# A two-block transformer program on one core: 28 weight pieces of the second block split ahead of time on POOL

## The chip, the core and the metric

The kernel runs on one core of one Trainium2 chip. The metric is the device time of one execution in microseconds (us). Five engines work side by side and wait for each other through semaphores: PE (TensorE: matrix products), DVE (VectorE: element-wise work), ACT (ScalarE: element-wise work and function tables), POOL (GpSimd: element-wise work, and transfers of its own) and SP (SyncE: only starts transfers). Each engine takes its instructions strictly in the order in which the built program holds them.

## What is computed

512 tokens with 1024 channels go through a first block of two layers (mixer, cross-attention, feed-forward with a convolution, each followed by a residual and a layer norm) and then through a second block. The second block, cut to what matters here:

```python
def second_block(x, c, norm_g, w_ada, b_ada, w_in, ...):
    mod = silu(c) @ w_ada + b_ada
    shift, scale, gate = split(mod, 3)
    h = rms_norm(x, norm_g) * (1 + scale) + shift
    proj = h @ w_in                      # r, k, v, g, wd+ad | q, ka, va, g_a
    ps = token_shift(proj[..., :D_SHIFT], mu_shift)
    y_r, g_r = rwkv7_mix(ps, ...)        # 8 heads, a state per head, 512 steps
    y_a = chunk_band_attention(q, ka, va, ...)
    y = concat(y_r * silu(g_r), y_a * silu(g_a))
    return x + gate * (y @ w_out)
```

All inputs are float32. A float32 product is made of three products of rounded parts: hi\*hi, hi\*lo and lo\*hi, where hi is the value cast to the engine's 32-bit format `fp32r` and lo is the value minus hi. So each weight has to be split into hi and lo before PE can use it.

## The kernel before

A weight matrix is cut into pieces of 128 x 1024 numbers (0.5 MB). `piece` (line 239) brings one in: SP loads it into a `raw` tile, ACT casts it to hi (line 229), and DVE, or in the second block POOL, subtracts to get lo (line 230). Hi and lo lie together in a tile `w` of 128 x 2 x 1024 (1 MB) from a ring of four; the first block has more rings (`rawx`, `wx`). A piece feeds 24 products of 512 columns (lines 263 to 265, three for each of 8 groups of channels).

The feed-forward stage `ffn` (line 619) runs over three chunks of hidden channels: 8, 8 and 6 blocks "up" (two pieces each), each followed by 8 blocks "down" (one piece each). In it DVE makes the splits of the weights and of the hidden values `hd`, and POOL has nothing to do until the residual's sums (`res_stat`, lines 370 and 371) at the end of the third chunk.

The second block has one line of work with long waits, and much other work for PE. The line is, for each of four pairs of heads, `rwkv_pair` (line 866), then the inversion of small triangular matrices `rwkv_invert` (line 990), then the chain of states `rwkv_chain`. The other work stands in the list `ORDER` (line 48): an entry is a milestone and a name, `r5` being piece 5 of the matrix `in_r`, `q17` the same for queries and keys, `g` the gates, `v0` and `v1` two passes over the four pieces of the values. `fill(us)` takes that much of it from the list wherever the line would wait; work of a later milestone isn't touched before the line has got there. Pieces 16, 0, 4, 8 and 1 (`OPEN`) are multiplied already in `open2`, ahead of the second block; `ORDER` names piece 1 once more as `r1`.

In `rwkv_pair` DVE works with POOL on the same tiles: line 904 (a scan) and 889 on DVE, 905 on POOL, 921, 892, 913 and 894 on DVE, 914, 919, 915 and 919 on POOL, then 918 on DVE. A PE product on the result of line 894 (line 897; it is recorded at line 834, that of the helper `mm`) follows, then transposes (837), the scores within the chunks (834), DVE's masks (960) and line 971. In `rwkv_invert` DVE runs 31 steps of two small instructions (lines 1003 and 1005), each on the result of the last, and then the result goes out to HBM and back (lines 1007 to 1020) before line 1027 turns it. The normalisation of queries and keys (lines 348 to 350, 1160, with a PE product at 1157) is mixed into these steps.

What follows is printed by a program, with the lines of the profile:

Of the kernel before, what the change touches and what calls it, by code (L numbers as in the profile page):

```python
# [172 lines left out]
class Prog:  # L173
# [69 lines left out]

    def raw(self):
# [7 lines left out]
    def wtile(self):  # L252
        """The weights' ring: some of its room is there only in the first block."""
# [13 lines left out]
    def lin(self, src, ms, xs, epi, n=S, first=0, last=0):  # L267
        """The first (last) few blocks go through one half of the tokens, then through the other, for the LN
        before (after) them; epi(m, psum, tokens) gets the last ones by halves."""
# [43 lines left out]
    def flush(self):  # L313
        """The LN that is due."""
# [6 lines left out]
    def lin_tm(self, src, pieces, xs, ntok, epi):  # L321
        """out[tok tiles][128, 512 cols]: activations stationary, weights moving."""
# [20 lines left out]
    def rsqrt(self, y, t, v, eps):  # L343
        """y = (v + eps) ** -0.5: the table's value and a Newton step; eps is a column of self.eps."""
# [7 lines left out]
    # residual, then LN over the channels  # L352
# [61 lines left out]
    # mixer of layer 0  # L414
# [204 lines left out]
    def ffn(self, l, xs):  # L619
        nc = self.nc  # L620
        for c, (f0, f1) in enumerate(CHUNKS):
# [3 lines left out]
            def epi(m, ps, ts):  # L625
# [9 lines left out]
                else:  # L635
                    h = self.tmp()
                    nc.vector.tensor_tensor(out=h, in0=ps, in1=keep["g"], op=ALU.mult)
                    hs.append(self.split(self.hd(), h))

# [5 lines left out]
            def epi_d(m, ps, ts):  # L645
# [5 lines left out]
                if c == 1 and l == 0 and m == 1:  # L651
                    self.ada_end()
                if c == 2:
                    self.res_stat(m, ts)
# [5 lines left out]
    # the modulation of the second block, gathered a piece at a time  # L660
# [23 lines left out]
    def ada_end(self):  # L684
        nc = self.nc
        # the sum over the partitions: within 32 of them by turning 32-blocks, then over the four groups
# [18 lines left out]
    def modulate(self, ts):  # L705
        """rms_norm(x) * norm_g * (1 + scale) + shift of half of the tokens."""
# [16 lines left out]
    def open2(self):  # L723
        """The second block's first products, of the first half of the tokens."""
# [48 lines left out]
    # The second block has one line of work with long waits (the states) and much other work for the tensor  # L773
    # engine: `bg` holds the latter as generators, and fill() puts some of it wherever the former waits.
# [57 lines left out]
    def mm(self, out, **kw):  # L832
        """A product on the line with the waits: it stays behind what fill() put before it."""
        self.tc.keep_in_program_order(self.nc.tensor.matmul(out, **kw))  # L834
# [4 lines left out]
    def lin_g(self, src, m, xs, epi, ks=range(KT)):  # L839
        w = self.piece(self.a[src][m])  # L840
# [25 lines left out]
    def rwkv_pair(self, j):  # L866
        """What the chunks of heads 2j and 2j+1 need."""
# [9 lines left out]
        # kk  # L877
# [12 lines left out]
        # k'  # L890
        nc.scalar.activation(u, av, AF.Identity, bias=self.ka1[:, j : j + 1], scale=self.v("k_a_2", j))
        nc.vector.tensor_tensor(out=k, in0=k, in1=u, op=ALU.mult)
        # bonus
# [7 lines left out]
        # decays  # L901
# [469 lines left out]
```

## Time and profile before

| | us |
|---|---|
| median of 3 runs | 1854.24 |
| the runs | 1853.18 to 1855.95 |
| the profiled execution (its span) | 1854.5 |
| PE busy | 1786.7 (96%) |
| DVE busy | 1096.3 (59%) |
| ACT busy | 783.0 (42%) |
| POOL busy | 362.8 (20%) |

The second layer's feed-forward stage lies between 1047 and 1430 us of the span, the four pairs between 1460 and 1600, the inversion between 1600 and 1661, and the chain of states and the output after that. A row of a timeline gives the start, the duration, the engine, the line, the operation, the output and input tiles, and in square brackets how long the engine had been idle and what ended that.

### The profile page before, as it was taken

To read this page: it belongs to the slowest core of one execution; us is meant where nothing else is said; L and a number is where in the kernel's file an instruction comes from. 1 tells how busy PE (TensorE), PEld (TensorE's weight loads), DVE (VectorE), ACT (ScalarE), POOL (GpSimd) and SP (SyncE) were. 2 spreads that over 40 slices of the span, in tenths; PEclk is the share of its full clock that TensorE was granted. 3 is DMA by queue.
4 is the path that set the end of the run, shared out by engine and by line. 5 is a ranking of instruction groups with operands and counts; after the bars stand their busy time and mean duration, and the time that the engine had idled before them with its cause. 6 is when DMAs were issued, how large, how long until landed. Compare 5 with 4: busy or idle time off the path is not lost.

```text
span 1854.5 us, 26344 instructions
## 1 busy us (share of the span) xinstructions
PE 1786.7 (96%) x10476; PEld 1502.4 (81%) x10476; DVE 1096.3 (59%) x1741; ACT 783.0 (42%) x1319; POOL 362.8 (20%) x331
## 2 busy tenths in 40 slices
PE   8999998999999999999999999999998888879999
PEld 7889988888888888988998988888887766656657
DVE  5676689743463467444565764343447666975673
ACT  5444534532332356232453642232335645535561
POOL 0115014000000051000501400000015455623232
PEclk9999999999999999999999999999999999989999
DMA  8431455332322226333131242323222222222142
GB/s 279 145 103 60 132 181 188 100 102 91 102 92 91 80 64 196 112 96 100 59 104 35 69 125 92 102 92 100 88 86 73 82 75 88 89 74 81 56 160 103
DMA packets 62635, 192.25 MB, mean 104 GB/s; under 512 B 7344, under 2 KB 10032, under 8 KB 62512
## 3 DMA queue, kind: packets, MB, share of 16 engines
q1 hardware_dynamic: 54432, 172.25, 29.0%
q0 software_dynamic: 3248, 9.44, 1.5%
q10 hardware_dynamic: 4832, 8.88, 1.4%
q8 instruction: 82, 1.34, 0.3%
q14 instruction: 41, 0.34, 0.1%
HBM read 181.36 MB, written 9.18 MB: 103 GB/s over the span
## 4 chain that ended last, share of the span: by engine, by line
PE 76%; DVE 15%; ACT 3%; issue 3%; DMA 2%; POOL 0%; SPq 0%; DVEq 0%; ACTq 0%; POOLq 0%
PE ch L264 10%; PE ch L263 10%; PE ch L265 10%; PE mm L263 9%; PE mm L265 9%; PE mm L264 9%; PE pv L264 3%; PE pv L263 3%; PE pv L265 3%; PE ch L834 3%; DVE x L401 2%; DVE xh L405 1%; DVE w L230 1%; DVE x L400 1%; DVE vt L681 1%
## 5 line engine op out<-in xcount | busy, mean ns | idle before, releaser
L263 PE MATMUL mm<-xh,w 128*128 128x512 f32 (+1 forms) x704 | 266.1, 378 | 8.5 <-ACT w L229 7.5
L265 PE MATMUL mm<-xh,w 128*128 128x512 f32 (+1 forms) x704 | 258.6, 367 | 0.8 <-DVE w L230 0.8
L264 PE MATMUL mm<-xh,w 128*128 128x512 f32 (+1 forms) x704 | 259.0, 368 | 0.0
L370 POOL TENSOR_TENSOR t<-x,x 128x512 f32<-128x512 f32 x6 | 8.1, 1351 | 1011.1 <-ACT w L229 656.1
L229 ACT CAST w<-raw 128x1024 fp32r<-128x1024 f32 (+2 forms) x131 | 133.1, 1017 | 164.0 <-PE ch L265 62.9
L263 PEld LDWEIGHTS mm<-xh,w 128*128 128x128 f32 x704 | 135.6, 193 | 35.7 <-ACT w L229 7.8
L264 PE MATMUL ch<-xh,w 128*128 128x512 f32 (+1 forms) x432 | 154.1, 357 | 0.6 <-DVE xh L405 0.5
L264 PEld LDWEIGHTS mm<-xh,w 128*128 128x128 f32 x704 | 135.9, 193 | 22.9 <-issue 3.4
L263 PE MATMUL ch<-xh,w 128*128 128x512 f32 (+1 forms) x432 | 153.0, 354 | 1.3 <-ACT xh L404 1.3
L265 PE MATMUL ch<-xh,w 128*128 128x512 f32 (+1 forms) x432 | 152.7, 353 | 1.5 <-DVE w L230 1.5
L265 PEld LDWEIGHTS mm<-xh,w 128*128 128x128 f32 x704 | 135.8, 193 | 22.6 <-issue 1.1
L229 ACT CAST wx<-raw 128x1024 fp32r<-128x1024 f32 (+1 forms) x85 | 88.1, 1039 | 152.4 <-PE ch L265 71.5
L230 DVE TENSOR_TENSOR w<-rawx,w 128x1024 fp32r<-128x1024 f32 (+2 forms) x85 | 104.1, 1225 | 68.0 <-ACT w L229 67.6
L229 ACT CAST w<-rawx 128x1024 fp32r<-128x1024 f32 (+2 forms) x85 | 87.3, 1027 | 116.4 <-PE mm L265 71.0
L230 DVE TENSOR_TENSOR w<-raw,w 128x1024 fp32r<-128x1024 f32 (+2 forms) x90 | 113.0, 1257 | 37.8 <-ACT w L229 37.4
L230 DVE TENSOR_TENSOR wx<-raw,wx 128x1024 fp32r<-128x1024 f32 (+1 forms) x85 | 107.6, 1267 | 27.6 <-ACT wx L229 27.4
L230 POOL TENSOR_TENSOR w<-raw,w 128x1024 fp32r<-128x1024 f32 x41 | 100.4, 2456 | 119.0 <-ACT w L229 115.1
L263 PE MATMUL ch<-xh,wx 128*128 128x512 f32 (+1 forms) x304 | 103.5, 341 | 0.0
L265 PE MATMUL ch<-xh,wx 128*128 128x512 f32 (+1 forms) x304 | 103.0, 339 | 0.0
L264 PE MATMUL ch<-xh,wx 128*128 128x512 f32 (+1 forms) x304 | 103.0, 339 | 0.0
L263 PE MATMUL mm<-hd,w 128*128 128x256 f32 (+1 forms) x304 | 97.7, 322 | 3.6 <-ACT hd L229 3.6
L265 PE MATMUL mm<-hd,w 128*128 128x256 f32 (+1 forms) x304 | 97.9, 322 | 0.0
(484 smaller groups left out, 4498.6 us busy)
## 6 DMA issues: line engine op xcount, KB each, us to landing
raw<-in_up SPq DMA_DIRECT2D x56, 512.0 KB, 3.5
rawx<-in_up SPq DMA_DIRECT2D x32, 512.0 KB, 3.5
kt<-in_ada SPq DMA_DIRECT2D x48, 256.0 KB, 3.3
raw<-in_dn SPq DMA_DIRECT2D x24, 512.0 KB, 3.5
raw<-in_in_r SPq DMA_DIRECT2D x24, 512.0 KB, 3.5
raw<-in_c_in SPq DMA_DIRECT2D x16, 512.0 KB, 3.5
raw<-in_xo SPq DMA_DIRECT2D x12, 512.0 KB, 3.6
raw<-in_xv SPq DMA_DIRECT2D x11, 512.0 KB, 4.1
```

Source lines behind the costliest of these rows:

```text
L229: nc.scalar.copy(hi, src)
L230: (eng or nc.vector).tensor_tensor(out=lo, in0=src, in1=f32(hi), op=ALU.subtract)
L263: mm(out, lhsT=ah, rhs=bh, start=start, stop=False)
L264: mm(out, lhsT=ah, rhs=bl, start=False, stop=False)
L265: mm(out, lhsT=al, rhs=bh, start=False, stop=stop)
L370: eng.tensor_tensor(out=sz, in0=self.x[0][:, ts] if m == 1 else sz, in1=z, op=ALU.add)
L400: (nc.vector if k in DVE_SUB else nc.gpsimd).tensor_tensor(out=x, in0=x, in1=mn, op=ALU.subtract)
L401: nc.vector.scalar_tensor_tensor(out=x, in0=x, scalar=gk, in1=rs, op0=ALU.mult, op1=ALU.mult)
L405: nc.vector.scalar_tensor_tensor(out=lo, in0=x, scalar=bk, in1=f32(hi), op0=ALU.add, op1=ALU.subtract)
L681: nc.vector.scalar_tensor_tensor(out=dst, in0=raw, scalar=sc, in1=dst, op0=ALU.mult, op1=ALU.add)
L834: self.tc.keep_in_program_order(self.nc.tensor.matmul(out, **kw))
```

## The change

1. `r1` is taken out of `ORDER`: piece 1 of `in_r` is multiplied once (in `open2`), not twice.
2. `pre_begin`, at the start of the second layer's feed-forward, lists 28 pieces in the order of `ORDER`: those of `r`, `q` and `g` that are left and the four of `v0`.
3. `pre_step` takes one of them, after each hidden block and after each "down" block of the first two chunks (32 calls). POOL copies one column of the tile just made by DVE into the new tile (which makes POOL wait for that point of the stage), starts the load, casts to hi, subtracts to lo, and starts the store of hi and lo (1 MB) to HBM. There are two tiles for it, under the tag `vt`, which cross-attention has finished with by then.
4. `ready` takes the place of `piece` in `lin_g`, `att_v`, `out_begin` and `out_end`: if the piece was prepared, SP loads the 1 MB straight into the `w` tile, and neither ACT nor POOL touches it. The pieces of the output matrix weren't prepared and go through `piece` as before.

```diff
 ORDER = (
-    (0, "r1"), (0, "r5"), (0, "r9"),
+    (0, "r5"), (0, "r9"),
...
+    def pre_step(self, at):
+        nc = self.nc
+        if self.todo:
+            key = self.todo.pop(0)
+            t = self.t("vt", [P, 2, D], F32, 2)
+            nc.gpsimd.tensor_copy(t[:, 1, 0:1], at[:, 0:1])
+            nc.gpsimd.dma_start(out=t[:, 1, :], in_=self.a[key[0]][key[1]])
+            self.due2.append((key, t))
+        if len(self.due2) > 1 or not self.todo:
+            for key, t in self.due2[:1]:
+                self.due2.pop(0)
+                hi, lo = t[:, 0, :].bitcast(F32R), t[:, 1, :].bitcast(F32R)
+                nc.gpsimd.tensor_copy(hi, t[:, 1, :])
+                nc.gpsimd.tensor_tensor(out=lo, in0=t[:, 1, :], in1=t[:, 0, :], op=ALU.subtract)
...
+                d = self.prep[key] = self.dram.tile([P, 2, D], F32, tag=name, name=name)
+                nc.gpsimd.dma_start(out=d, in_=t)
...
+    def ready(self, src, m):
+        if (src, m) not in self.prep:
+            return self.piece(self.a[src][m])
+        w = self.wtile()
+        self.nc.sync.dma_start(out=f32(w), in_=self.prep[src, m])
+        return w
...
@@ ffn
                     hs.append(self.split(self.hd(), h))
+                    if l == 1:
+                        self.pre_step(f32(hs[-1][:, 0, :]))
...
+                if c < 2 and l == 1:
+                    self.pre_step(x)
...
@@ lin_g
-        w = self.piece(self.a[src][m])
+        w = self.ready(src, m)
```

POOL in the second pair of heads. `w` and `raw` are a piece and its source; `rt`, `rk`, `ar` and `c` are the pair's own tiles; `yd` and `dn` are in HBM. Before:

```order
L230 TENSOR_TENSOR w_12628<-raw_12627,w_12628 128x1024
L905 TENSOR_TENSOR rt_12460<-rt_12462,rt_12460 128x512
L230 TENSOR_TENSOR w_12667<-raw_12666,w_12667 128x1024
L914 TENSOR_TENSOR ar_12520<-rk_12297,rt_12516 128x8x64
L919 TENSOR_TENSOR c_1638_12521<-rk_12349,rt_12462 64x8x64
L915 TENSOR_TENSOR rt_12484<-rt_12484,rt_12461 128x512
L919 TENSOR_TENSOR c_1638_12521<-rk_12349,rt_12462 64x8x64
L230 TENSOR_TENSOR w_12690<-raw_12689,w_12690 128x1024
L900 DMA yd<-rt_12463 128x512
```

The same place on POOL after the change (lines 905, 914, 919, 915, 900 and 966 are now 952, 961, 966, 962, 947 and 1013):

```order
L952 TENSOR_TENSOR rt_12615<-rt_12617,rt_12615 128x512
L961 TENSOR_TENSOR ar_12672<-rk_12408,rt_12668 128x8x64
L966 TENSOR_TENSOR c_1658_12673<-rk_12490,rt_12617 64x8x64
L962 TENSOR_TENSOR rt_12636<-rt_12636,rt_12616 128x512
L966 TENSOR_TENSOR c_1658_12673<-rk_12490,rt_12617 64x8x64
L947 DMA yd<-rt_12618 128x512
L1013 DMA dn<-mk_1600_12387 32x8x32 x4
```

The three subtractions of weight pieces are gone from among the pair's own five instructions.

PE in the first pair of heads, from the product on line 894's result on: `mm_12359` is a filler product of `r9`, `at` and `ch` are the scores. Before:

```order
L834 MATMUL ch_12271<-rt_12225,cst 128x512
L837 MATMUL ch_12314<-cst,rk_12207 64x128
L834 MATMUL ch_12314<-cst,rk_12207 64x64
L837 MATMUL ch_12314<-cst,rk_12207 128x128 x3
L837 MATMUL ch_12332<-cst,rk_12207 128x128 x4
L264 MATMUL mm_12359<-xh_11312,w_12355 128x512
L265 MATMUL mm_12359<-xh_11312,w_12355 128x512
L263 MATMUL mm_12359<-xh_11313,w_12355 128x512
```

The same place on PE after the change (834 and 837 are now 881 and 884):

```order
L881 MATMUL ch_12464<-rt_12421,cst 128x512
L884 MATMUL ch_12504<-cst,rk_12403 64x128
L881 MATMUL ch_12504<-cst,rk_12403 64x64
L884 MATMUL ch_12504<-cst,rk_12403 128x128 x3
L884 MATMUL ch_12522<-cst,rk_12403 128x128 x4
L881 MATMUL at_12545<-ar_12475,c_1624_12476 128x128
L881 MATMUL ch_12544<-ar_12475,c_1624_12476 128x128
```

Eight filler products stood between the transposes and the first scores, and 18 more between and after the scores; now there are none, and 7 after the scores. Ahead of this place 45 filler products stand where 46 stood.

SP at the beginning of the second block. Before:

```order
L241 DMA raw_12469<-in_in_r 128x1024
L241 DMA raw_12540<-in_in_r 128x1024
L241 DMA raw_12596<-in_in_va 128x1024
L241 DMA raw_12627<-in_in_va 128x1024
L241 DMA raw_12666<-in_in_va 128x1024
```

The same place on SP after the change (`sp_...` is a prepared piece in HBM):

```order
L282 DMA w_12495<-sp_in_r_9528 128x2048
L282 DMA w_12624<-sp_in_r_9605 128x2048
L282 DMA w_12692<-sp_in_r_9682 128x2048
L282 DMA w_12745<-sp_in_va_9759 128x2048
L282 DMA w_12773<-sp_in_va_9836 128x2048
```

The loads go straight into the ring `w`, so a load waits until PE has left the tile; before it waited until POOL had left one of two `raw` tiles.

## Rows read from the trace of the kernel before

**Rows 1.** The page: busy time of each engine, its share of the span, instructions.

```profile
PE 1786.7 (96%) x10476; PEld 1502.4 (81%) x10476; DVE 1096.3 (59%) x1741; ACT 783.0 (42%) x1319; POOL 362.8 (20%) x331
```

**Rows 2.** Busy time of each engine in stretches (the clock is 1.00 at 2.4 GHz).

```profile
core 0: us, PE busy (x) PEld busy (x) DVE busy (x) ACT busy (x) POOL busy (x), PEclk, DMA share, GB/s
0.00:46.00 46.00, 37.77 (x235) 35.28 (x236) 25.23 (x43) 24.44 (x37) 0.51 (x5) 0.96 0.83 278
1060.00:1300.00 240.00, 239.39 (x1114) 199.05 (x1113) 111.72 (x133) 83.11 (x107) 0.00 (x0) 1.00 0.31 99
1460.00:1600.00 140.00, 120.30 (x687) 87.71 (x686) 99.52 (x140) 72.64 (x103) 85.92 (x57) 0.93 0.25 79
1600.00:1661.00 61.00, 50.21 (x200) 37.11 (x196) 53.80 (x94) 23.20 (x33) 24.33 (x21) 0.89 0.31 96
1661.00:1855.00 194.00, 186.47 (x1558) 126.81 (x1557) 107.79 (x325) 91.49 (x218) 46.93 (x36) 1.00 0.28 97
```

**Rows 3.** What PE waited for from 1437 us on: total, times, longest.

```profile
PE ch L834 <- DVE rt L894: 17.8, 4, 4.9
PE at L1157 <- ACT t L1153: 6.0, 2, 5.8
PE ch L834 <- DVE rt L1027: 3.3, 1, 3.3
```

**Rows 4.** PE's timeline in the first pair: fillers, then the product on line 894.

```profile
1465.42 0.40 PE L263 MATMUL mm<-xh,w 128*128 128x512 f32 x1
...
1474.28 0.39 PE L263 MATMUL mm<-xh,w 128*128 128x512 f32 x1
1479.34 1.47 PE L834 MATMUL ch<-rt,cst 128*128 128x512 f32 x2 [4.67 <-DVE rt L894]
```

**Rows 5.** DVE's timeline in the second pair and, last row, in the fourth.

```profile
1503.87 2.25 DVE L921 COPY pc<-rt 128x8 f32<-128x8 f32 x1
1506.04 0.68 DVE L892 TENSOR_TENSOR rk<-rk,rt 128x512 f32<-128x512 f32 x1
...
1508.31 2.96 DVE L894 SCALAR_TENSOR_TENSOR rt<-rk,vec,rk 128x512 f32<-128x512 f32 x1
...
1581.44 2.68 DVE L892 TENSOR_TENSOR rk<-rk,rt 128x512 f32<-128x512 f32 x1
```

**Rows 6.** POOL's timeline at the same places.

```profile
1503.23 2.86 POOL L230 TENSOR_TENSOR w<-raw,w 128x1024 fp32r<-128x1024 f32 x1
1506.04 1.79 POOL L914 TENSOR_TENSOR ar<-rk,rt 128x512 f32<-128x512 f32 x1
...
1580.74 2.83 POOL L230 TENSOR_TENSOR w<-raw,w 128x1024 fp32r<-128x1024 f32 x1
```

**Rows 7.** DVE's lines 349 and 1003 from 1600 to 1652 (min/median/max ns), and two timelines.

```profile
L349 DVE TENSOR_SCALAR t<-t x5: 420/428/4366, 1604.4 to 1651.3; 128x512 f32<-128x512 f32 x5
...
L1003 DVE TENSOR_TENSOR rt<-c,c x31: 191/374/2514, 1609.4 to 1646.9; 128x31 f32<-128x31 f32 x2, 128x60 f32<-128x60 f32 x2, 128x87 f32<-128x87 f32 x2, 128x112 f32<-128x112 f32 x2
...
1610.95 2.33 DVE L1003 TENSOR_TENSOR rt<-c,c 128x87 f32<-128x87 f32 x1
...
1610.74 4.79 POOL L230 TENSOR_TENSOR w<-raw,w 128x1024 fp32r<-128x1024 f32 x2 [2.28 <-ACT w L229]
```

**Rows 8.** Groups of instructions from 1437 us on (first row), and from 1060 to 1300.

```profile
L230 POOL TENSOR_TENSOR w<-raw,w 128x1024 fp32r<-128x1024 f32 x40 | 97.8, 2454 | 118.1 <-ACT w L229 114.3 <-DMA raw<-in_in_r 3.5
...
L230 DVE TENSOR_TENSOR w<-raw,w 128x1024 fp32r<-128x1024 f32 x16 | 19.6, 1223 | 3.7 <-ACT w L229 3.7
...
L230 DVE TENSOR_TENSOR hd<-t,hd 128x512 fp32r<-128x512 f32 x16 | 11.0, 685 | 0.7 <-ACT hd L229 0.7
```

**Rows 9.** Transfers: SP's queue from 1060 to 1300; KB and us to landing from 1437.

```profile
q1 hardware_dynamic: 6480, 23.60, 30.6%
...
raw<-in_in_r SPq DMA_DIRECT2D x18, 512.0 KB, 3.5
...
dt<-c POOLq DMA_DIRECT2D x1, 512.0 KB, 2.9
```

More of the change, by code (lines that the diff above doesn't have):

```diff
@@ L242, in piece, with pre_begin @@
         return self.split(w, raw[:, :cols], cols, None if self.extra else self.nc.gpsimd)
+    def pre_begin(self):
+        self.prep, todo = {}, []
+        for _, ws in ORDER:
+            for w in ws.split("+"):
+                k, m = w[0], int(w[1:])
+                if k in "rq" and m not in OPEN:
+                    todo.append(("in_r", m))
+                elif k == "g":
+                    todo.append(("in_r", 12 + m) if m < 4 else ("in_ga", m - 4))
+                elif w == "v0":
+                    todo += [("in_va", i) for i in range(4)]
+        self.todo, self.due2 = todo, []
+    def pre_step(self, at):
[12 more added lines that the diff above has]
+                nc.gpsimd.tensor_tensor(out=lo, in0=t[:, 1, :], in1=t[:, 0, :], op=ALU.subtract)
+                name = f"sp_{key[0]}{key[1]}"
+                d = self.prep[key] = self.dram.tile([P, 2, D], F32, tag=name, name=name)
[6 more added lines that the diff above has]
+        return w
     def raw(self):
@@ L620, in ffn @@
         nc = self.nc
+        if l == 1:
+            self.pre_begin()
         for c, (f0, f1) in enumerate(CHUNKS):
@@ L638, in epi @@
                     hs.append(self.split(self.hd(), h))
+                    if l == 1:
+                        self.pre_step(f32(hs[-1][:, 0, :]))
             self.lin(f"up{l}", [o + f for f in range(f0, f1) for o in (NF, 0)], xs, epi, first=FIRST if c == 0 else 0)
@@ L1133, in att_v @@
         for jj in range(4):
-            w = self.piece(self.a["in_va"][jj])
+            w = self.ready("in_va", jj)
             for kk in range(2):
@@ L1257, in out_begin @@
         for m in range(NPART):
-            w, ps = self.piece(self.a["out"][m]), self.bank(("mm", "mm", "ch", "ch")[m])
+            w, ps = self.ready("out", m), self.bank(("mm", "mm", "ch", "ch")[m])
             self.part.append((w, ps))
@@ L1276, in out_end @@
             else:
-                w, ps = self.piece(self.a["out"][m]), self.bank()
+                w, ps = self.ready("out", m), self.bank()
                 for k in range(KT):
```

## The prediction

> **What bounds the kernel now.** I read the busy times first: PE works 96% of the span and no other engine comes near [rows 1], so time can only go where PE is idle, slow, or does work it need not do. The stretches show where that is [rows 2]. In the second layer's feed-forward (1060 to 1300) PE has no gap and POOL does nothing. In the four pairs (1460 to 1600) PE is idle for 140.0 - 120.3 = 19.7 us, in the inversion (1600 to 1661) for 10.8 us. After 1661 it is nearly full until the output's last pieces, which the change doesn't touch. The granted clock fell in just these two stretches, behind the waits: a mean of 0.93 over 140 us is a loss of 9.8 us of full-speed work, 0.89 over 61 us one of 6.7 us; each is time at the level of 1.2 GHz in place of 2.4. Idle time and clock together are 47 us, the most that any cure of the waits could bring.
>
> Then what ended the waits [rows 3]: four times DVE's line 894, at most 4.9 us each, once each in a pair; in the inversion ACT's line 1153 (5.8 us) and line 1027. All belong to the line of work in the second block, none to a weight piece. So pieces arrive in time already, and the split can matter only by what it does to DVE and ACT. The timelines show that it does: DVE's line 921, a copy of eight columns, took 2.25 us and ended at 1506.12, when POOL's split of a weight piece ended at 1506.09 [rows 5, 6]. Line 892 took 0.68 us in the second pair, but 2.68 in the fourth, where such a split ran from 1580.74 on. In the inversion a step of 87 columns took 2.33 us beside two splits, where the median step, a longer one, takes 0.374 [rows 7]. DVE stands still for as long as POOL works on a piece. POOL does this 40 times from 1437 us on, 2.45 us each [rows 8]; the change leaves the 8 pieces of the output matrix.
>
> **The change part by part.** *Piece r1.* 24 products go. Fillers follow each other every (1474.28 - 1465.42)/39 = 0.227 us [rows 4], so PE has 5.4 us less. They go from the first pair: behind the product on line 894, 7 fillers stand where 26 stood. Ahead of it the number is the same, so nothing of this is lost in the wait. But what follows (masks, line 971) is DVE's own line, and with fewer fillers PE may meet it: between 2 and 5.4 us, I take 4.4, since the splits that held DVE there are gone too.
>
> *The splits leave the pairs.* One split per pair stands between line 904 and line 894: ahead of line 921 in three pairs, of line 892 in the fourth. Each costs the line about 2.0 us (2.68 - 0.68 for line 892; for line 921 2.25 less a small copy, near the 0.191 of the smallest step in [rows 7]). POOL's own lines stay, and line 914 moves up into the place of the split: it took 1.79 us against 2.86 [rows 6], so at least 2.86 - 1.79 = 1.07 us is gained, at most 2.86. I take 2.0, four times: 8 us (4.3 to 11.4). Each is less than its wait, so all of it shows, and POOL's lines 919 and 915, inside line 894's 2.96 us, are next late: they stay.
>
> *The splits leave the inversion.* Five of the 62 steps took 2.3 to 2.6 us, 12.2 us together, where five median ones take 5 x 0.37: 10.4 us too long. Line 349 took 4.37 us ahead of the first step, 0.43 in the median [rows 7]: 3.9 us. The steps form one chain, so 14.3 us can go. PE's work up to line 1027's products is 163 fillers, 163 x 0.227 = 37 us, and a few small products, in a stretch of 61, so PE doesn't bound this before the chain does. The result's way through HBM (2.9 us out [rows 9], as much back) now runs beside loads of 1 MB. If each way took 2.9 us longer, 8.5 would be left; and if the port went to others in half the cases, 5. I take 12 (5 to 14.3); the 5.8 us behind ACT's line 1153 goes with it, since ACT stood there behind DVE.
>
> *The clock.* Of the 16.5 us, what follows waits that become short comes back. Waits of line 894 shrink from 4.9 to some 2.5 us; whether the clock then falls, no row tells: 0 to 10 us, and I take 4.
>
> *Work for POOL in the feed-forward.* Each piece adds a cast and a subtraction of 128x1024, two transfers that POOL issues, and a one-column copy. The subtraction is the 2.45 us of [rows 8]; no row has POOL's cast, which lies between nothing and another 2.45 us. 28 x 4.9 = 137 us at most. DVE in these 240 us has 111.7 us of work [rows 2], of which the splits of weights (45 in three groups, one of them in [rows 8], at 1.22) and of hidden values (16 at 0.69), 66 us together, are of the kind that stood still. Were all this strictly one after the other, 137 + 111.7 = 249 us would be 9 us more than PE's 240. But pieces are split several ahead of PE, and POOL would have to use its whole bound: 0 to 9 us lost, I take 1, for the two turns from up to down, where the last hidden block is split just ahead of its use. That POOL itself falls behind costs nothing: the 28th call comes with the fourth down block of the second chunk, and its next own work, the residual's sums, stands 16 more pieces for PE later, 16 x 5.4 = 87 us.
> Here the Trainium skill has a rule that speaks against the change (SBUF — State Buffer, "Who interferes with whom"): a DVE instruction with two inputs in SBUF and a GpSimd instruction that reads SBUF take one shared port pair in turn, held for the whole instruction. By it the 66 us are the ones that wait; line 892's two durations agree. The page GPSIMD Engine Reference ("Engine selection") says that one-input work runs at roughly line rate; by that the cast would be about half of the subtraction, an estimate of 1.2 us, and the sum 28 x 3.7 + 111.7 = 215 us, with no loss at all.
>
> *Transfers.* POOL moves 28 x 1.57 MB = 44 MB beside SP's 23.6 MB [rows 9]. That sum, 68 MB in 240 us, would be 282 GB/s; the densest stretch of the trace moved 278, with the transfer engines 83% busy [rows 2]. SP's part is 98 GB/s and needs less than half of that: cost 0, see the rivals. In the second block a load is 1 MB, not 0.5: it lands between the 3.5 us of half a megabyte and twice that, 7.0 us. It starts when PE leaves the tile and is needed three pieces later, 3 x 5.4 = 16 us, or three quarter passes of v0 or v1, 3 x 2.7 = 8 us. It fits, narrowly for the values: 0 to 4 us lost, I take 1. ACT loses 32 casts, which I put at nothing: its casts stood between table functions of the same line, and shortening them moves what DVE already delays.
>
> *Sum.* 4.4 + 8 + 12 + 4 - 1 - 1 = 26.4 us off the profiled 1854.5 us, 1828 us. The median of the runs, 1854.24, is the same to 0.02%.
>
> **The rivals.** *The port is given back* (mechanism right, gain small): POOL's own lines 905, 914, 919 and 915 fill the places of the splits and hold DVE nearly as long, and the inversion ends in the wait for its transfers. Against it: five steps of the inversion have no other POOL work near them. With 3 us of r1, 4 of the pairs and 4 of the inversion, less 1, it gives 1845 us.
>
> *Slower: SP's loads starve in the feed-forward.* If POOL's transfers take their places by size, SP's rows of 4 KB stand against POOL's 4 KB read and 8 KB written: a quarter of 278 GB/s, 70 GB/s. POOL's 44 MB then last 44/208 = 210 us, in which SP moves 14.7 MB instead of the 20.6 that PE needs; the missing 5.9 MB at 98 GB/s are 60 us. 1828 + 60 = 1888 us. It decides from the point at which SP's rate falls below 23.6 MB in 240 + 26 us, 89 GB/s. For it speaks that 278 is all that the trace shows; against it that POOL has only two tiles, waits for each transfer, and so leaves gaps to SP.
> The Trainium skill (DMA: Bandwidth & Descriptors, "Issuing engines are not separate DMA queues") says that transfers run on the same 16 engines and interleave whoever started them; by that the sharing is real. No row here has both queues full.
>
> *It doesn't do what it says:* the prepared pieces change no wait, and only r1 counts, eaten in part by the feed-forward: 1854.5 - 4.4 + 2 = 1852 us.
>
> **How the numbers follow.** The forecast 0.70, the port given back 0.20, starved loads 0.06, nothing but r1 0.04. The forecast's own bounds are best 5.4 + 11.4 + 14.3 + 10 = 41 us (1813) and, since the low ends won't meet, about 12 us less than the sum of 26.4 (1840). The range reaches over the port's case as well, 1812 to 1846, and leaves out the last two and some of the tails. A measurement of this kernel can tell about 0.2%, 3.7 us, from no change: faster 0.90 (the first two), same 0.04, slower 0.06.
>
> **What would show it.** Right: in the pairs line 921 under 2 us or held by line 914 and no longer by a split, PE's four waits for line 894 near 2.5 us, no step of lines 1003 and 1005 over 0.5 us, the stretch from line 1011's first fill to line 1027 about 12 us shorter, PE still full from 1060 to 1300 with POOL about half busy. Wrong: PE waiting for ACT's or DVE's splits in the feed-forward (starved loads), or for a transfer into w in the second block; line 894 still ending waits of over 4 us (the port given back); a longer wait at line 1027 that eats the inversion's gain.

## The result

The changed kernel takes 1828.4 us (median of 4 runs, 1826.4 to 1832.9) against 1855.0 us for the kernel before (1853.2 to 1856.0): a ratio of 0.9859, 95% interval 0.9842 to 0.9877. A second measurement beside other kernels gave 1827.4 us, 0.9856 (0.9840 to 0.9871). The forecast was 1828 us. The total hides misses of several microseconds that partly cancel: new loads that slow a transfer on the critical line, and casts on ACT that were put at nothing. The experiments found both.

The page of the changed kernel, the line that answers [rows 1]:

```profile
PE 1771.9 (97%) x10452; PEld 1493.4 (82%) x10452; DVE 1099.3 (60%) x1739; ACT 751.3 (41%) x1285; POOL 425.7 (23%) x438
```

PE has 24 products fewer and 14.8 us less busy time, and the span is 29.8 us shorter: half of the gain is idle time of PE that is gone. The stretches, as in [rows 2]; the last row is the four pairs as they lie now, from the first pair's first product to the inversion's first step:

```profile
1060.00:1300.00 240.00, 239.39 (x1108) 198.75 (x1107) 139.81 (x131) 81.79 (x103) 109.42 (x107) 1.00 0.67 234
1460.00:1600.00 140.00, 129.09 (x741) 96.62 (x740) 102.64 (x178) 59.03 (x91) 42.22 (x41) 0.96 0.44 161
...
1456.70:1585.60 128.90, 118.00 (x693) 87.43 (x693) 91.18 (x145) 58.06 (x87) 42.22 (x41) 0.96 0.43 155
```

In the feed-forward PE is as full as before, to the hundredth, although POOL is now busy there for 109 us and DVE for 140 in place of 112. In the pairs POOL's busy time is halved and PE's clock is 0.96 in place of 0.93.

What PE waited for from 1420 us on, as in [rows 3]:

```profile
PE ch L881 <- DVE rt L941: 10.1, 4, 2.9
PE ch L881 <- DVE rt L1074: 6.1, 1, 6.1
PE at L757 <- ACT kt L449: 2.7, 1, 2.7
```

Line 941 is the old 894: its four waits fell from 17.8 to 10.1 us. The 5.8 us behind ACT's line 1153 are gone. But the wait for line 1074, the old 1027, has doubled. DVE's timeline in the second pair and, last row, in the fourth, as in [rows 5]:

```profile
1493.87 1.26 DVE L968 COPY pc<-rt 128x8 f32<-128x8 f32 x1
1495.05 0.68 DVE L939 TENSOR_TENSOR rk<-rk,rt 128x512 f32<-128x512 f32 x1
1495.65 0.68 DVE L960 SCALAR_TENSOR_TENSOR ar<-rt,rt 128x512 f32<-128x512 f32 x1
1496.25 2.96 DVE L941 SCALAR_TENSOR_TENSOR rt<-rk,vec,rk 128x512 f32<-128x512 f32 x1
...
1563.68 2.98 DVE L941 SCALAR_TENSOR_TENSOR rt<-rk,vec,rk 128x512 f32<-128x512 f32 x1
```

In the fourth pair before, the same line (894) took less:

```profile
1584.16 1.63 DVE L894 SCALAR_TENSOR_TENSOR rt<-rk,vec,rk 128x512 f32<-128x512 f32 x1
```

POOL's at the same place, as in [rows 6]:

```profile
1493.35 1.75 POOL L961 TENSOR_TENSOR ar<-rk,rt 128x512 f32<-128x512 f32 x1
1495.87 1.57 POOL L966 TENSOR_TENSOR c<-rk,rt 64x512 f32<-64x512 f32 x1 [0.77 <-DVE rk L939]
1497.41 1.25 POOL L962 TENSOR_TENSOR rt<-rt,rt 128x512 f32<-128x512 f32 x1
```

Line 968 (921 before) is down from 2.25 to 1.26 us, and what holds it is POOL's own line 961: both end at 1495.1. Line 941 still takes 2.96 us, across POOL's lines 966 and 962. The first of the two lines of the inversion's steps (count, ns min/median/max, first and last start), as in [rows 7]:

```profile
L1050 DVE TENSOR_TENSOR rt<-c,c x31: 191/358/426, 1585.6 to 1612.5; 128x31 f32<-128x31 f32 x2, 128x60 f32<-128x60 f32 x2, 128x87 f32<-128x87 f32 x2, 128x112 f32<-128x112 f32 x2
```

The result's way out to HBM and back, POOL's timeline:

```profile
1613.21 0.55 POOL L1054 DMA_DIRECT2D dt<-c  x1 [33.16 <-DVE c L1052]
1620.63 1.61 POOL L1062 DMA_DIRECT2D c<-dt  x2 [6.87 <-DMA dt<-c]
```

DVE's timeline, where it comes back:

```profile
1625.30 1.29 DVE L1074 STREAM_TRANSPOSE rt<-c 32x512 f32<-32x512 f32 x2 [6.19 <-DMA c<-dt]
```

The inversion's two large transfers, in and out (queue, KB, us to landing):

```profile
c<-dn POOLq DMA_DIRECT2D x1, 512.0 KB, 6.1
dt<-c POOLq DMA_DIRECT2D x1, 512.0 KB, 6.8
```

No step is over 0.43 us any more, and the steps last from 1585.6 to 1612.9, 27.3 us; before they lasted 37.9 (1609.4 to 1647.3). But the write of the result (`dt<-c`) landed after 6.8 us; before it was 2.9 [rows 9]. The inversion's input (`c<-dn`) took 6.1, before 3.6.

Cutting the span at four points that every trace shows gives the table on which the rest goes (all from the profiled executions, in us):

| | start to pair 1 | pair 1 to the first step | the steps | last step to line 1074 | line 1074 to the end | span |
|---|---|---|---|---|---|---|
| before | 1460.6 | 148.8 | 37.9 | 7.4 | 199.9 | 1854.5 |
| after | 1456.7 | 128.9 | 27.3 | 12.4 | 199.4 | 1824.7 |
| r1_only | 1455.5 | 144.6 | 37.8 | 7.3 | 199.1 | 1844.2 |
| unused | 1459.9 | 141.8 | 39.9 | 7.2 | 199.3 | 1848.1 |
| after, second profile (`after_again`) | 1452.3 | 131.3 | 27.3 | 12.8 | 199.9 | 1823.6 |
| split_only | 1456.5 | 138.5 | 27.3 | 9.8 | 199.2 | 1831.3 |
| act_late | 1453.1 | 136.6 | 27.3 | 12.2 | 197.9 | 1827.2 |
| lo_late | 1464.5 | 143.9 | 41.3 | 10.4 | 201.2 | 1861.3 |
| gate_dt | 1455.5 | 128.9 | 27.3 | 7.3 | 198.3 | 1817.3 |
| pool_own | 1453.2 | 130.3 | 29.0 | 11.4 | 204.5 | 1828.4 |
| both | 1458.5 | 130.0 | 29.0 | 10.9 | 197.9 | 1826.3 |
| both2 | 1452.1 | 128.1 | 29.0 | 7.1 | 195.7 | 1812.0 |
| best | 1453.8 | 120.4 | 29.0 | 7.0 | 196.7 | 1806.9 |
| best2 | 1453.9 | 117.6 | 29.0 | 6.8 | 197.1 | 1804.4 |

The first column differs by some microseconds between profiles even where nothing was changed ahead of it (after had 1456.7 in one execution and 1452.3 in another), so the columns behind it tell more than the spans, and the medians more than single profiles. The second column of after itself differs by 2.4 us between its two profiles, so smaller differences there mean nothing.

### The profile page after: what moved, and what is told of

The parts are those of the page before. It is cut to its first block, busy times and chain, and to the rows that moved or that the text cites. A ratio compares the mean times of both kernels' runs of the same rounds, so it can differ in the third digit from the quotient of the medians.

```text
span 1824.7 us, 26404 instructions
## 1 busy us (share of the span) xinstructions
PE 1771.9 (97%) x10452; PEld 1493.4 (82%) x10452; DVE 1099.3 (60%) x1739; ACT 751.3 (41%) x1285; POOL 425.7 (23%) x438
## 4 chain that ended last, share of the span: by engine, by line
PE 78%; DVE 13%; ACT 3%; DMA 3%; issue 2%; POOL 0%; SPq 0%; DVEq 0%; ACTq 0%; POOLq 0%
PE ch L305 10%; PE ch L304 10%; PE ch L306 10%; PE mm L304 9%; PE mm L305 9%; PE mm L306 9%; PE pv L305 4%; PE pv L304 3%; PE pv L306 3%; PE ch L881 3%; DVE x L442 1%; DVE xh L446 1%; DVE w L230 1%; DVE x L441 1%; PE at L1229 1%
## 5 line engine op out<-in xcount | busy, mean ns | idle before, releaser
L304 PE MATMUL mm<-xh,w 128*128 128x512 f32 (+1 forms) x696 | 260.4, 374 | 6.4 <-ACT w L229 6.2
L306 PE MATMUL mm<-xh,w 128*128 128x512 f32 (+1 forms) x696 | 253.9, 365 | 0.8 <-DVE w L230 0.8
L305 PE MATMUL mm<-xh,w 128*128 128x512 f32 (+1 forms) x696 | 254.2, 365 | 0.0
L304 PEld LDWEIGHTS mm<-xh,w 128*128 128x128 f32 x696 | 132.7, 191 | 33.1 <-ACT w L229 6.8
L229 ACT CAST w<-raw 128x1024 fp32r<-128x1024 f32 (+2 forms) x98 | 98.7, 1008 | 145.9 <-PE ch L306 63.6
L305 PEld LDWEIGHTS mm<-xh,w 128*128 128x128 f32 x696 | 132.8, 191 | 22.6 <-issue 3.5
L306 PEld LDWEIGHTS mm<-xh,w 128*128 128x128 f32 x696 | 132.9, 191 | 21.5 <-DVE w L230 1.0
L230 DVE TENSOR_TENSOR w<-rawx,w 128x1024 fp32r<-128x1024 f32 (+2 forms) x85 | 110.2, 1296 | 63.4 <-ACT w L229 62.9
L230 DVE TENSOR_TENSOR w<-raw,w 128x1024 fp32r<-128x1024 f32 (+2 forms) x90 | 123.8, 1376 | 37.7 <-ACT w L229 37.1
L230 DVE TENSOR_TENSOR wx<-raw,wx 128x1024 fp32r<-128x1024 f32 (+1 forms) x85 | 119.6, 1409 | 30.4 <-ACT wx L229 30.0
L229 ACT CAST w<-rawx 128x1024 fp32r<-128x1024 f32 (+2 forms) x85 | 87.3, 1027 | 110.0 <-PE mm L306 69.9
L304 PE MATMUL mm<-hd,w 128*128 128x256 f32 (+1 forms) x304 | 98.0, 323 | 3.6 <-ACT hd L229 3.6
L306 PE MATMUL mm<-hd,w 128*128 128x256 f32 (+1 forms) x304 | 98.3, 323 | 0.0
L305 PE MATMUL mm<-hd,w 128*128 128x256 f32 (+1 forms) x304 | 97.6, 321 | 0.0
```

The costliest lines, as they stand in the source:

```text
L229: nc.scalar.copy(hi, src)
L230: (eng or nc.vector).tensor_tensor(out=lo, in0=src, in1=f32(hi), op=ALU.subtract)
L304: mm(out, lhsT=ah, rhs=bh, start=start, stop=False)
L305: mm(out, lhsT=ah, rhs=bl, start=False, stop=False)
L306: mm(out, lhsT=al, rhs=bh, start=False, stop=stop)
```

## The experiments

### The two halves of the change

`r1_only` is the kernel before with one line changed:

```diff
-    (0, "r1"), (0, "r5"), (0, "r9"),
+    (0, "r5"), (0, "r9"),
```

> The kernel before with one edit of the change alone: r1 leaves the fillers of pair 1, so that its 24 matmuls run with the open-block pieces and nothing is split ahead. Theory (the splits' hold on the port is the larger part of the gain, r1 the smaller): 4.4 us less than before, 1850 us (1848 to 1853); the four waits for L894 stay, at 17 to 18 us together, and the inversion keeps its five steps of over 2.3 us. Rival (r1's place in the list is what brings the gain, the prepared pieces only move work): 1828 to 1835 us, with the inversion's slow steps gone though POOL still splits there. Second rival (pair 1 fills up with another piece, so nothing is saved): 1854 to 1856 us.

Measured: 1848.0 us against 1855.3 (ratio 0.9961, 0.9945 to 0.9977), 7.2 us less with an interval of 4.3 to 10.2. The waits and the inversion are as expected:

```profile
PE ch L834 <- DVE rt L894: 18.3, 4, 5.3
```

All five slow steps are still there (2.33 to 2.55 us). So the prepared pieces are worth 1848.0 - 1828.4 = 19.6 us, and r1 alone 7.2. The other way round, `split_only` is the kernel after with `(0, "r1")` put back.

> The kernel after with r1 put back into pair 1, where it is now loaded ready-made (29 prepared pieces in place of 28). Theory (the two parts add up): the gain of r1 alone is lost again, 4.4 us of it, 1832 to 1833 us (1830 to 1835). Rival (r1 was long only because its own piece was split there, and costs nothing once it is prepared): 1828 us, the same as after. Second rival (the prepared pieces bring little without r1's going): over 1845 us.

Measured: 1833.1 us (0.9878, 0.9864 to 0.9893), 4.7 us above after. The parts add up within the noise: r1 is worth 7.2 us (4.3 to 10.2) taken alone and 4.7 taken last. The intervals of `split_only` and after overlap slightly, so the time alone doesn't rule out that a prepared r1 costs nothing; the table speaks against it, with 138.5 us in the second column where after has 128.9 and 131.3.

### What the work in the feed-forward costs

`unused` does all of the change's work in the feed-forward stage and leaves the result unread:

```diff
-        if (src, m) not in self.prep:
+        if True:
             return self.piece(self.a[src][m])
```

> The kernel after with the prepared pieces left unread: the last feed-forward stage casts, subtracts and stores the 28 pieces as in after, and the second block loads and splits the raw pieces as before. It tells the price of the work in the feed-forward stage, against the kernel before without r1. Theory (PE stays full there, POOL and the DMA have room): 0 to 1 us above r1 alone, 1850 to 1852 us, and no wait of PE for w in the stage over 1 us. Rival (the port and the 28 MB of stores and 14 MB of loads slow DVE's own splits and SP's loads enough to be felt): 4 to 10 us above r1 alone, 1855 to 1861 us, with waits for w or hd between 1060 and 1373 us.

Measured: 1848.5 us (0.9963, 0.9947 to 0.9978), 0.5 us above `r1_only`, with intervals that overlap nearly whole: nothing that can be told from zero. The groups of the changed kernel between 1060 and 1300 us (count, busy us, mean ns, idle before) show how it is paid for:

```profile
L272 POOL TENSOR_TENSOR vt<-vt 128x1024 fp32r<-128x1024 f32 x21 | 51.4, 2447 | 1.5
L230 DVE TENSOR_TENSOR w<-raw,w 128x1024 fp32r<-128x1024 f32 x16 | 29.4, 1835 | 3.6 <-ACT w L229 3.6
...
L271 POOL CAST vt<-vt 128x1024 fp32r<-128x1024 f32 x21 | 26.2, 1246 | 79.5 <-DMA vt<-in_in_r 51.8 <-DMA vt<-in_in_va 27.6
...
L230 DVE TENSOR_TENSOR hd<-t,hd 128x512 fp32r<-128x512 f32 x16 | 14.3, 894 | 0.7 <-ACT hd L229 0.7
```

DVE's splits of the same shape rose from 1223 to 1835 ns and from 685 to 894 [rows 8]: DVE paid 28 us in this stretch for POOL's 78 us of casts and subtractions. PE didn't notice: its longest wait from 1060 to 1373 us is 0.5 us, for ACT, in after and in `unused` alike. That the pieces are split several ahead of PE is the likely reason. POOL mostly waited for its own loads.

### POOL's subtraction or ACT's cast

The change takes two things out of the second block's line at once: POOL's subtraction and ACT's cast. Two kernels put them back one at a time. `lo_late` stores hi and the raw piece in HBM and subtracts after the load:

```diff
@@ pre_step
-                nc.gpsimd.tensor_tensor(out=lo, in0=t[:, 1, :], in1=t[:, 0, :], op=ALU.subtract)
@@ ready
         self.nc.sync.dma_start(out=f32(w), in_=self.prep[src, m])
+        self.nc.gpsimd.tensor_tensor(out=w[:, 1, :], in0=f32(w[:, 1, :]), in1=f32(w[:, 0, :]), op=ALU.subtract)
```

> The kernel after, but POOL does the subtraction of the prepared pieces in the second block again: in the last feed-forward stage only the cast is done, the rounded piece and the raw one are stored, and behind each 1 MB load POOL subtracts in place. What stays as in after: no ACT cast, no raw buffer, 1 MB loads, r1 gone. Theory (POOL's subtraction, two inputs from SBUF, holds DVE off the port they share): most of the gain of the pairs and of the inversion goes back, 1843 to 1850 us, the inversion's steps of over 2.3 us are there again beside L282's row on POOL, and the waits for L941 add up to 16 or more. Rival (the gain came from ACT's casts, the raw ring or the loads, which are all still as in after): 1827 to 1832 us. Between 1833 and 1842: both.

Measured: 1856.5 us (1.0006, 0.9994 to 1.0018). All of the gain is gone, r1's too, which is more than expected. DVE's timeline in the inversion:

```profile
1612.76 0.36 DVE L1050 TENSOR_TENSOR rt<-c,c 128x192 f32<-128x192 f32 x1
1613.15 2.44 DVE L1052 TENSOR_TENSOR c<-c,rt 128x192 f32<-128x192 f32 x1
1615.62 2.45 DVE L1050 TENSOR_TENSOR rt<-c,c 128x207 f32<-128x207 f32 x1
1618.11 2.56 DVE L1052 TENSOR_TENSOR c<-c,rt 128x207 f32<-128x207 f32 x1
1620.70 0.39 DVE L1050 TENSOR_TENSOR rt<-c,c 128x220 f32<-128x220 f32 x1
```

POOL's beside it:

```profile
1612.92 4.92 POOL L282 TENSOR_TENSOR w<-w 128x1024 fp32r<-128x1024 f32 x2 [8.03 <-DMA w<-sp_in_r]
1618.06 2.38 POOL L282 TENSOR_TENSOR w<-w 128x1024 fp32r<-128x1024 f32 x1 [0.22 <-DMA w<-sp_in_r]
```

Three subtractions of POOL, three steps of DVE that last as long as they do: with no ACT cast of these pieces, five steps are over 2 us again. So POOL's subtraction alone holds them. The Trainium skill names a port for it in SBUF — State Buffer, "Who interferes with whom": a DVE instruction with two inputs in SBUF contends with a GpSimd instruction that reads SBUF, and the port pair that they share is an exclusive lock. These rows agree: 2.44 to 2.56 us beside POOL, 0.36 and 0.39 just before and after. The table tells why the kernel lost r1's gain too: the steps take 41.3 us and the result's way through HBM 10.4, for the 1 MB loads stayed. Without the free port, the prepared loads in this form are a loss of 8.5 us against `r1_only`.

`act_late` puts ACT's cast back alone:

```diff
         self.nc.sync.dma_start(out=f32(w), in_=self.prep[src, m])
+        self.nc.scalar.copy(w[:, 0, :], f32(w[:, 0, :]))
```

> The kernel after with ACT's cast put back alone: behind each prepared 1 MB load ACT copies the rounded half onto itself, 32 copies of about 1.2 us, and PE's matmuls of the piece wait for it; POOL stays free. Theory (ACT's casts were worth nothing, the gain is POOL's subtraction): 1828 to 1831 us, waits for L941 at 9 to 12 us together, no slow step in the inversion. Rival (ACT's casts held up the pairs' tanh, square and exp and so carried part of the gain): 1835 us or more, with L941's waits longer.

Measured: 1833.0 us (0.9891, 0.9863 to 0.9919), 4.6 us above after, between the two theories; the intervals of the two ratios overlap, so the time alone doesn't settle it. The waits do:

```profile
PE ch L882 <- DVE rt L942: 13.9, 4, 3.8
```

With POOL free and ACT casting, the four waits are 13.9 us; with ACT free and POOL subtracting (`lo_late`) they are 14.8; with both busy (`r1_only`) 18.3, with neither (after) 10.1. Each carries about 4 us of them, and these sums hardly vary between profiles (10.1 in both of after, 9.9 in `split_only`; 17.8 before, 18.4 in `unused`). ACT's timeline in the first pair of `act_late` shows how:

```profile
1457.80 0.72 ACT L388 ACTIVATE rt<-rt,eps 128x512 f32<-128x512 f32 x1
1458.43 1.03 ACT L283 CAST w<-w 128x1024 fp32r<-128x1024 f32 x1
1459.37 0.63 ACT L389 ACTIVATE rt<-rt 128x512 f32<-128x512 f32 x1
```

DVE's timeline behind it, first in `act_late`, then (line 389) in after:

```profile
1460.03 0.69 DVE L390 SCALAR_TENSOR_TENSOR rt<-rt,rt 128x512 f32<-128x512 f32 x1 [2.59 <-ACT rt L389]
```

```profile
1462.50 0.69 DVE L389 SCALAR_TENSOR_TENSOR rt<-rt,rt 128x512 f32<-128x512 f32 x1 [1.45 <-ACT rt L388]
```

The cast stands between two functions of the line, and DVE waits 1.14 us longer for the second. The inversion's steps are 27.3 us with ACT's casts, as in after: there only POOL counts. In the table's second column the two don't add up: `lo_late`, with POOL's subtraction alone, has 143.9 us, as much as `r1_only`; `act_late` has 136.6, 5.3 to 7.7 above after.

### Where 5 us of the gain went

Between the last step and line 1074 after needs 12.4 us in place of 7.4. At 1612.75, 0.46 us ahead of the write of the result, SP had started a prepared load of 1 MB (`in_r` 24). `gate_dt` holds this load until the result is back:

```diff
         w = self.wtile()
+        if (src, m) == ("in_r", 24):
+            with self.tc.high_priority(offset=HPG):
+                self.nc.vector.tensor_copy(w[64:96, 0, 0:1], self.td[64:96, 0:1])
         self.nc.sync.dma_start(out=f32(w), in_=self.prep[src, m])
```

`td` is the tile into which the result comes back.

> The kernel after with one 1 MB load (in_r 24) held back until the inversion's result has come back from HBM: a 32x1 copy on DVE from that result into the piece's buffer stands ahead of the load. Theory (the 5 us that the result's way through HBM grew by, 12.1 us in place of 7.1 from the inversion's last step to the first transposition, are this load's share of the DMA engines): dt<-c lands in about 3 us again, and the run takes 1823 to 1825 us. Rival (the small rows of the write are slow in this place whatever runs beside them, or PE's fillers are the limit): 1827 to 1830 us. Second rival (the held load comes too late for PE): 1830 to 1834 us, with a wait for w between 1630 and 1650 us.

Measured: 1823.1 us (0.9828, 0.9800 to 0.9856). In its trace the write, in POOL's timeline:

```profile
1612.00 0.55 POOL L1058 DMA_DIRECT2D dt<-c  x1 [33.13 <-DVE c L1056]
1615.51 1.61 POOL L1067 DMA_DIRECT2D c<-dt  x2 [2.95 <-DMA dt<-c]
```

and what PE waited for behind it:

```profile
PE ch L885 <- DVE rt L1079: 1.0, 1, 1.0
```

2.95 us in place of 6.87, and the table's fourth column is 7.3 again, with the second and third columns unchanged to 0.1 us. The medians are 5.3 us apart; their intervals still overlap a little, but the row that was to move moved by what was expected. So the loads cost the line 5 us: 3.9 in the write, beside `in_r` 24, and most of the rest in the way back (`c<-dt`, 4.7 us to landing against 3.3 in `gate_dt`), beside the load that followed at 1619.18 us. `split_only` shows the same by chance: there the load had started 3.2 us ahead of the write in place of 0.46, and the write took 3.5 us.

### What still holds line 941

`pool_own` moves the pairs' own five instructions from POOL to DVE (`nc.gpsimd` becomes `nc.vector` on lines 952, 961, 962 and 966).

> The kernel after with the pairs' own five POOL instructions (L952, L961, L962 and L966 twice, 1.3 to 1.7 us each) moved to DVE, where the like takes 0.66 to 0.69. Theory (what still holds L941 at 2.98 us in every pair is POOL's own work on the shared port): L941 takes 0.7 us, PE's four waits for it fall from 10.1 us together to 2 to 5, and the run takes 1820 to 1824 us. Rival (DVE has 3.3 us more to do in every pair and is itself the chain, so nothing is won): 1827 to 1833 us, with L941 at 0.7 us but started later.

Measured: 1827.7 us (0.9857, 0.9828 to 0.9885), no gain. But line 941 did what was expected, as DVE's timeline in the second pair shows:

```profile
1490.45 0.75 DVE L941 SCALAR_TENSOR_TENSOR rt<-rk,vec,rk 128x512 f32<-128x512 f32 x1
```

PE's waits:

```profile
PE ch L881 <- DVE rt L1074: 7.3, 1, 7.3
PE mm L304 <- issue: 3.6, 1, 3.6
...
PE ch L881 <- DVE rt L941: 1.5, 3, 0.5
```

The waits for line 941 fell from 10.1 to 1.5 us, and two others took their place. DVE's timeline in pair 3 tells what the one without a releaser ("issue") is:

```profile
1524.38 0.74 DVE L815 SCALAR_TENSOR_TENSOR rk<-mm,mu,t 128x511 f32<-128x511 f32 x1
...
1533.39 0.20 DVE L817 TENSOR_SCALAR rk<-mm,mu 128x1 f32<-128x1 f32 x1
```

PE's timeline there:

```profile
1533.69 0.47 PE L304 MATMUL mm<-xh,w 128*128 128x512 f32 x1 [3.58 <-issue]
```

Lines 815 and 817 read one finished PSUM bank between them, 511 columns and one. The one column was 9 us late, behind the pair's longer list on DVE, and the bank was free only then. The other is again the way through HBM: 7.2 us for the write. This profile also lost time to the clock at its end: from 1724 us on the granted clock was 0.94, where after has 1.00 in its last 99 us, and the last column is 204.5. The third column, 29.0 here and in the kernels built on this one, holds one group of the normalisation's instructions more (after's lines 389 to 391 and 1207).

`both` joins `pool_own` and `gate_dt`.

> The two edits together, the held load and the five instructions on DVE. Theory (they act in different places): the sum of both gains, 1815 to 1820 us. Rival (PE is full in between, so one gain eats the other): no lower than the better of the two.

Measured: 1828.5 us (0.9858, 0.9841 to 0.9876). The theory fell: no sum, not even the better of the two. The held load had slipped behind the next one in SP's order, and that one (`in_r` 14) started at 1617.62, just ahead of the write at 1617.78, which took 6.97 us:

```profile
1625.30 1.61 POOL L1067 DMA_DIRECT2D c<-dt  x2 [6.97 <-DMA dt<-c]
```

In `gate_dt` the same load was started after the write had landed, by luck of when PE left the tile.

### Taking the two new waits away

Three kernels were timed together with after, unchanged.

> The kernel after, unchanged, timed beside the next three on the same chip: 1826 to 1831 us.

It took 1827.4 us (0.9856, 0.9840 to 0.9871). `both2` is `both` with SP's loads kept in the program's order:

```diff
-        self.nc.sync.dma_start(out=f32(w), in_=self.prep[src, m])
+        self.tc.keep_in_program_order(self.nc.sync.dma_start(out=f32(w), in_=self.prep[src, m]))
```

> The held load and the five instructions on DVE as before, and SP's prepared loads kept in the order in which the program asks for them, so that in_r 14 stands behind the held in_r 24 and cannot be in flight beside the inversion's write (it was issued 0.16 us ahead of it in the run before). Theory (the gain of DVE's part was there and went into the result's way through HBM, 10.6 us with in_r 14 beside it, 7.0 without): 1822 to 1825 us, dt<-c in about 3 us. Rival (the way is long in that place for another reason): 1827 to 1830 us, as before.

Measured: 1817.5 us (0.9806, 0.9784 to 0.9828), 10 us under after and 11 under `both`, more than expected; the write takes 2.95 us and the way 7.1. Of the 11 us, the way gives 3.8; what the rest is, single profiles don't settle (the pairs and the end are each about 2 us shorter than in `both`). The 3.6 us of PE in pair 3 are still there. `best` takes those away too:

```diff
@@ shift
-        nc.vector.tensor_scalar(out=out[:, 0:1], in0=ps[:, 0:1], scalar1=mu1, scalar2=None, op0=ALU.mult)
+        nc.scalar.activation(out[:, 0:1], ps[:, 0:1], AF.Copy, scale=mu1)
```

> The run before, and the column that shift writes apart (L817 in after, 128x1 from the PSUM bank) moved from DVE to ACT. Theory (PE's 3.6 us of waiting in pair 3 ended with that instruction, which stood 9 us behind its partner on DVE and held the bank): the wait goes, 2 to 4 us less than the run before, 1818 to 1822 us. Rival (the bank is held by something else, or the next piece waits for its load then): the same as the run before.

Measured: 1808.9 us (0.9761, 0.9742 to 0.9780), below both kernels with room to spare: 46 us under before and 19 under after. The pairs, from the first product to the first step, read as follows:

```profile
1453.80:1574.10 120.30, 118.33 (x716) 88.56 (x716) 83.36 (x156) 60.82 (x98) 12.21 (x21) 1.00 0.51 183
```

PE is idle for 2.0 us of 120.3 where it was idle for 10.9 of 128.9 in after, and the mean granted clock is 1.00. The gain over `both2` is 8.7 us, more than the 3.6 us of the one wait. The traces show the larger part of it: PE's waits for lines 945 (1.5 us) and 970 (1.4) are gone as well, and its idle time in this stretch falls from 8.5 us to 2.0. Why these two went, no run takes apart.

`best2` also holds `in_r` 22 until the inversion's input has landed, in the manner of `gate_dt`.

> The run before, and in_r 22 held until the inversion's input has landed (c<-dn took 6 to 7 us with 1 MB loads beside it, 3.6 in the kernel before). Theory (the inversion starts 2.5 to 3.5 us earlier and PE, which waited for its result, takes it up): 1816 to 1820 us. Rival (PE then waits for in_r 22 instead, or is full anyway): the same as the run before within 1 us.

Measured: 1811.8 us (0.9767, 0.9752 to 0.9782), the same as `best`. Its steps start 2.6 us earlier in the profile (1571.5 in place of 1574.1), and the runs don't show it. PE is nearly full there already, so I take it that this line no longer bounds the stretch.

## Why the prediction was right, and which of its terms were not

**What bounds the kernel.** Right: DVE's line in the pairs and in the inversion, and POOL's splits hold it in both. `lo_late` puts the subtraction back and loses the whole gain. What was missing is that in the pairs ACT's casts hold it too.

**r1, 4.4 us (2 to 5.4).** Right as far as the runs tell: 4.7 us taken last, and 7.2 taken alone, with an interval (4.3 to 10.2) that holds the term. In the second column, where r1 lies, `r1_only` is 4.2 us shorter than before.

**The splits leave the pairs, 8 us, and the clock, 4.** The size was about right. From pair 1 to line 1011's first fill (1058 after), the kernel before takes 140.0 us, `r1_only` 136.4 and after 121.5 (124.0 in its second profile): 12.4 to 14.9 us less than `r1_only`, where the two terms say 12. The clock's share of it, reckoned as in the prediction, is 9.8 us of loss before and 5.2 after (0.96 over 128.9 us), so about 4.6 in the pairs. The cause was only in part the one named. The waits for line 894 fell by 7.7 us, and about 4 of that was ACT's casts, which the prediction put at nothing ("shortening them moves what DVE already delays"). That step failed: by the rows of `act_late` it is DVE that waits for ACT, 2.59 us with the cast and 1.45 without. POOL's part of the waits, 4.4 to 4.7 us, was smaller than the 8 priced, because its own lines moved up into the holes: line 968 is held by line 961 for 1.1 to 1.3 us in three pairs, and in pair 4 line 941 takes 2.98 us where it took 1.63 before. So the rival "the port is given back" is true in part. As the prediction said, line 941 stayed next late; PE's four waits for it are 2.5 us each in the mean, the sign that was named.

**The splits leave the inversion, 12 us (5 to 14.3).** The steps are 10.6 us shorter, as worked out from the five slow ones. Line 349's 4.37 us are gone as well, but DVE then waited 2.4 us for the inversion's input from HBM, which landed in 6.1 us where it had taken 3.6. The sign that the prediction gave, a stretch from line 1011's first fill to line 1027 that is about 12 us shorter, did not come. It begins in DVE's timeline before at

```profile
1600.58 0.91 DVE L1011 MEMSET mk<- 32x1024 f32 x1 [0.27 <-issue]
```

after at

```profile
1578.25 0.91 DVE L1058 MEMSET mk<- 32x1024 f32 x1 [0.27 <-issue]
```

and in `gate_dt` at

```profile
1577.05 0.91 DVE L1063 MEMSET mk<- 32x1024 f32 x1 [0.27 <-issue]
```

so it lasts 54.1 us before, 47.1 after and 41.9 in `gate_dt`. After gained 7.0 us; with the load held it is 12.1, the term as priced. So the splits' worth was right, and the transfers took 5 us of it. That PE doesn't bound the stretch before the chain does held: it stood waiting for line 1074.

**Loads, 1 us (0 to 4).** This is the step that failed. It asked whether the 1 MB loads come in time for PE, and they do: no wait for a load stands among PE's. It did not put a price on what they do to the line's own transfers, though the inversion's paragraph had named it ("if each way took 2.9 us longer"). The write took 4 us longer, the way as a whole 5.0 us, and the input 2.5 us: `gate_dt` gets the 5 back. The longer wait at line 1027, which the prediction gave as a sign of being wrong, came in part: 6.1 us where it was 3.3. The right risk stood there as a lower bound of one term, and was left out of the sum.

**The feed-forward, 1 us (0 to 9).** Right as far as the runs tell: 0.5 by `unused`. POOL was busy for 109 of 240 us, "about half". The cast took 1.246 us, half of the subtraction's 2.447. The Trainium skill (GPSIMD Engine Reference, "Engine selection") says that one-input work runs at roughly line rate; the estimate of 1.2 us that the prediction made of it agrees with the trace. The rival of starved loads didn't come: SP's queue (`q1`) moved the same 23.60 MB as in [rows 9] beside POOL's (`q0`). Its loads landed later, after 4.3 to 5.7 us (medians by tile) in place of 3.5, and PE didn't wait for them. Queue, packets, MB, share:

```profile
q0 software_dynamic: 5950, 32.36, 38.0%
q1 hardware_dynamic: 6480, 23.60, 28.9%
```

**The sum.** From pair 1 to line 1074 after is 25.5 us shorter than before; the terms that lie there (4.4, 8, 12, 4 and -1) say 27.4. Up to the first fill it gained 18.4 us (15.9 by its second profile) where 16.4 was said, from there on 7.0 (6.8) where 11 was. So the point of 1828 us owes something to luck: what the way through HBM took was made up partly in the pairs, where ACT's share stood in for POOL's, and partly ahead of pair 1, where after's profiles are 3.9 and 8.3 us shorter than before's and no term says why. What the working had earned was the range, not the point.

## What to carry to other kernels

When a prepared copy takes the place of work done on the spot, look at the small transfers for which the critical line waits, beside the new, larger loads: a load that is in time for its own reader can still cost that line microseconds. Holding the load until the transfer is back brought them back here. Moving work off an engine pays only once what it hid is followed to the next holder: here the port, then a PSUM bank freed by a one-column instruction, then the order of SP's queue, each of which took up some of the gain of the edit before. Price every engine that the removed work ran on, not only the one whose rows look guilty.

## What the runs showed of the hardware that was not expected

A load of 1 MB that started 0.1 to 0.8 us ahead of a write of 512 KB stretched the write from 2.9 us to landing to between 6.3 and 7.2 (both profiles of after, `act_late`, `lo_late`, `pool_own`, `both`).

DVE did not always get a turn between two POOL instructions that followed each other. Line 941 started at 1496.25, inside POOL's line 966 (to 1497.44), and ended at 1499.2, after line 962 (to 1498.66): 2.96 us for 0.75 of work. But in `lo_late` three steps of the inversion ended 0.2 us after one subtraction each, the first of them between two subtractions without a gap, and in the fourth pair before line 894 took 1.63 us and got its turn between lines 914 and 919. What decides, no run shows.

On POOL a copy of one column is not free; the 128x1 copies that tie it to the feed-forward's pace took 366 and 434 ns:

```profile
L264 POOL COPY vt<-hd 128x1 f32<-128x1 f32 x14 | 5.1, 366 | 27.9 <-ACT hd L229 15.0 <-DMA sp_in_r<-vt 10.1 <-ACT w L229 2.7
...
L264 POOL COPY vt<-x 128x1 f32<-128x1 f32 x8 | 3.5, 434 | 15.9 <-DMA sp_in_r<-vt 15.9
```
